# Copying the own bank first: ScalarE's copy and VectorE's add change places in a Strassen-Winograd MLP on Trainium2

## The chip, the cores and the metric

The kernel runs on one NeuronCore of a Trainium2 chip. The engines of that core are TensorE (PE, matmuls; PEld is its weight load), VectorE (DVE), ScalarE (ACT), GpSimd (POOL) and SyncE (SP), and 16 DMA engines move data. The metric is the device time of one execution in microseconds; lower is better. "Before" is the kernel as it stood, "after" the changed one.

## What is computed

One inference step of a two-layer decoder trunk: 1024 prompt tokens and 8 sample tokens, width 1024. Layer 0 mixes tokens with a recurrent block, layer 1 with sliding-window attention; each is followed by an MLP of width 4096. The change lies in the MLP, which is most of the time:

```python
D_MODEL = 1024
D_FF = 4 * D_MODEL
...
def sq_relu_mlp(x, w_up, w_down):
    return jnp.square(jax.nn.relu(x @ w_up)) @ w_down
...
        yp = yp + sq_relu_mlp(rms_norm(yp, norm_mlp_g[layer]), mlp_w_up[layer], mlp_w_down[layer])
        ys = ys + sq_relu_mlp(rms_norm(ys, norm_mlp_g[layer]), mlp_w_up[layer], mlp_w_down[layer])
```

All is float32, and each product is made of three passes over a high and a low part of both operands.

## The kernel before

The 1032 tokens (T, padded) lie along the free axis, two halves of 516 (H0, H1). The MLP is written as 2x2 block products after Strassen and Winograd, with seven products in place of eight: the four blocks are even and odd row tiles of the output (tiles he and ho, in the code e and o) by the two token halves (e0, e1, o0, o1). `mlp_products` runs through a list of steps (kind, q, i): "up" pairs q = 0 to 15 of the first matmul of the MLP, then "dn" pairs of the second one, 20 per layer. A down pair covers one pair of output tiles and one chunk of the hidden tiles (`CHUNKS`, five chunks, of 3, 3, 3, 3 and 2 pairs of hidden tiles, four down pairs each). Two further pairs of hidden tiles are kept out of the scheme and done as a plain product at the end of each layer (the tail, `down_steps`, with matmuls at L226 and weights split at L165 and L166).

In each pair the products come in the order P1, P2, P6, P7, P5, P4, P3 (`ORDER`). `product` (L514 to L522) issues 24 matmuls for an up product, 18 or 12 for a down product, each 128x128 by 258 columns, into a double bank of PSUM. There are four double banks: two "G" in turn, one "X", one "Y". P1, P6, P5 and P3 of a pair accumulate in the pair's G, the shared banks, and after each of them the running sum is needed. P2 has Y to itself, P7 has X to itself, and P4 accumulates on top of P7 in X. What must be taken out of PSUM, per pair:

- L616, ScalarE: after P1 e0 <- G, after P6 o0 <- G, after P5 o1 <- G, after P3 e1 <- G.
- L618, VectorE: after P2 e0 += Y. L620, VectorE: after P5 o1 += X (that is P7). L624, VectorE: after P4 o0 += X.

P3 overwrites the sum in G that the copy after P5 reads, and P4 overwrites the P7 in X that the add at L620 reads. So in the kernel before, P3 must wait for the copy and P4 for the add.

The order of instructions on each engine is not written out: a scheduler fills each queue from the program, by readiness as it estimates it. `tc.high_priority()` draws an instruction forward (the copies at L616), and `tc.issue_after(last["copy"])` holds back the instructions in its block until the copy that was last recorded in `last["copy"]` has been placed.

Around the products other work shares the engines:

- weights: DMA on SP's queue (raw <- w_up or w_dn, L159), differences of weight tiles on VectorE (ws, L487), split into high and low part by ScalarE (L388) and VectorE (L389);
- in the down phase the sums of hidden tiles (hsum, in memory) are loaded by POOL's queue (tl <- hsum, L532, in `Ahead.fetch`) and split by ScalarE (cast, L394) and VectorE (subtract, L395) in `Ahead.split`, which stands under `issue_after(last["copy"])`. A chunk has 7 such tiles per pair of hidden tiles, fetched while the chunk before is computed;
- a finished down tile is added to memory by POOL (spill <- ho and spill <- he, L635, accumulating DMAs); in the last chunk the sum is added into the tile instead (ho <- spill, he <- spill, L637);
- for the tail, four hidden tiles of 1032 columns (loaded as hdl, split into hdh and hdl at L394 and L395) and four weight tiles (raw <- w_dn, then wh at L165 and wl at L166). The buffer of a raw tile comes free after its subtract at L166, and then SP issues the next load.

Of the kernel before, what the change touches and what calls it, by code (L numbers as in the profile page):

```python
# [13 lines left out]
ALU = mybir.AluOpType  # L14
# [45 lines left out]
def trunk(ctx: ExitStack, tc: tile.TileContext, I, O):  # L60
    nc = tc.nc
    pe, act, dve, pool, sp = nc.tensor, nc.scalar, nc.vector, nc.gpsimd, nc.sync
# [53 lines left out]
    def quarters(x):  # L116
        return x.rearrange("p (b c) -> p b c", b=2)

    def inner(d):
        return quarters(d)[:, :, 0:QT]  # L120
# [458 lines left out]
    def mlp_products(layer, tok, pw, r, spill, acc, gnext, after):  # L579
# [11 lines left out]
        for n, (kind, q, i) in enumerate(PROG):  # L591
# [13 lines left out]
            z = st[q]  # L605
# [3 lines left out]
            d = z["g"] if i in (1, 5, 6) else z[7] if i == 4 else z.get(i, z["g"])  # L609
            product(d, alone, wt, (tok if up else ahead).ops[x] if up else ahead.ops[q // 4][x])  # L610
            e, o, g = z["e"], z["o"], inner(z["g"])
            e0, e1, o0, o1 = [quarters(t[:, h]) for t in (e, o) for h in (H0, H1)]
            if i in (1, 6, 5) or i == 3:
                t, f = {1: (e0, g), 6: (o0, g), 5: (o1, g), 3: (e1, inner(d))}[i]
                with tc.high_priority():
                    last["copy"] = act.copy(t, f).ins  # L616
            if i == 2:
                dve.tensor_tensor(e0, inner(d), e0, ALU.add)  # L618
            elif i == 5:
                dve.tensor_tensor(o1, inner(z[7]), o1, ALU.add)  # L620
                if 3 in z:
                    dve.tensor_tensor(e1, g, e1, ALU.add)
            elif i == 4:
                dve.tensor_tensor(o0, inner(d), o0, ALU.add)  # L624
            ready = {4: "o", 3: "" if alone else "e", 5: "e" if 3 in z else ""}.get(i, "")
            if ready and up:
                t = z[ready]
# [4 lines left out]
            elif ready:  # L632
                m, t = 2 * (q % 4) + (ready == "o"), z[ready]
# [577 lines left out]
    def mlp(layer, r, spill, gnext, after):  # L1211
        swap_banks(f"pu{layer}")
        return mlp_products(layer, rs.pop("tok"), rs.pop(layer), r, None, spill, gnext, after)
# [147 lines left out]
```

## Time and profile before

| | us |
|---|---|
| median of 3 runs | 2075.74 (2073.16 to 2076.03) |
| profiled execution | 2076.53 |
| its span, first to last instruction | 2074.7 |
| TensorE busy in it | 2027.6 |
| up pairs of layer 0 and 1 | about 299 and 300 |
| down pairs of layer 0 and 1 | about 289 and 284 |
| tails | about 17 and 20 |

The mean granted clock of TensorE was 0.993 of full speed. In the slices of the page TensorE is at nine tenths or more nearly throughout. In the two up phases (380 to 679 us and 1426 to 1726 us) and the two down phases (679 to 968 and 1726 to 2010) its busy time is within 1 us of the stretch, since the ends of matmuls are modelled; a late start shows as a longer group of matmuls, and in the waits of the weight load (PEld). A timeline row reads: start, length from the first start to the last end of a group, engine, line, operation, out <- in, shapes, count, and in brackets how long the engine was idle before and what released it.

### The profile page before, as it was taken

What the parts mean: (1) busy time and instruction counts of PE and PEld (TensorE: products, weight loads), DVE (VectorE), ACT (ScalarE), POOL (GpSimd) and SP (SyncE); (2) the same over time, 40 slices, a digit from 0 to 9 for tenths busy, and PEclk for the clock granted to TensorE, in tenths of its full rate; (3) what the DMA queues carried; (4) which work ended last, traced back from release to release, by engine and by line L of the source; (5) the groups of instructions that cost most, each with busy time, mean ns of one, the idle gap of its engine ahead of it and who ended that gap; (6) DMA issues with size and microseconds to landing.
All of it is one profiled execution on the core that took longest, in us unless ns stands there. A gap on an engine that the chain in (4) does not pass through costs nothing.

```text
span 2074.7 us, 38720 instructions
## 1 busy us (share of the span) xinstructions
PE 2027.6 (98%) x15190; PEld 1986.7 (96%) x15190; DVE 1449.6 (70%) x2626; ACT 1093.9 (53%) x2157; POOL 382.1 (18%) x578
## 2 busy tenths in 40 slices
PE   6999999999999999999999998999999999999989
PEld 5999999999999999999999997999999999999989
DVE  6988537876766877766747878669676667676662
ACT  5476635543434655544447878545443446555450
POOL 4553100000001233221003444000000002323210
PEclk9999999999999999999999999999999999999999
DMA  5103142244436778868332322712443446887773
GB/s 172 51 14 71 53 160 86 103 147 144 147 134 213 217 205 221 228 156 202 113 87 71 93 59 79 232 59 87 165 149 133 157 170 227 223 226 204 172 183 103
DMA packets 112982, 296.48 MB, mean 143 GB/s; under 512 B 19992, under 2 KB 45088, under 8 KB 112800
## 3 DMA queue, kind: packets, MB, share of 16 engines
q1 hardware_dynamic: 56800, 127.01, 20.3%
q0 software_dynamic: 28352, 98.30, 18.2%
q10 hardware_dynamic: 27648, 68.70, 9.1%
q8 instruction: 119, 1.95, 0.4%
q14 instruction: 63, 0.52, 0.1%
HBM read 172.03 MB, written 109.25 MB: 136 GB/s over the span
## 4 chain that ended last, share of the span: by engine, by line
PE 88%; DVE 4%; ACT 3%; issue 2%; DMA 2%; POOL 1%; SPq 0%; ACTq 0%; DVEq 0%; POOLq 0%
PE bD L519 57%; PE bP L226 11%; PE bS L226 6%; PE bP L747 4%; PE bT L226 3%; PE bO L875 2%; PE bS L830 1%; PE bT L851 1%; PE bN L693 1%; PE bS L775 1%; DVE xc L1114 1%; DMA raw<-w_dn 1%; DVE wl L166 1%; DVE t L307 0%; DMA x<-xT 0%
## 5 line engine op out<-in xcount | busy, mean ns | idle before, releaser
L519 PE MATMUL bD<-op,op 128*128 128x258 f32 x5376 | 654.1, 283 | 1.4 <-ACT ho L616 1.4
L519 PEld LDWEIGHTS bD<-op,op 128*128 128x128 f32 x5376 | 649.0, 189 | 6.2 <-ACT ho L616 5.7
L519 PE MATMUL bD<-tl,op 128*128 128x258 f32 x4704 | 580.5, 285 | 8.8 <-ACT ho L616 8.8
L519 PEld LDWEIGHTS bD<-tl,op 128*128 128x128 f32 x4704 | 572.4, 190 | 16.6 <-ACT ho L616 15.8
L532 POOL DMA_DIRECT2D tl<-hsum x196 | 118.7, 738 | 850.6 <-ACT op L388 781.5
L389 DVE TENSOR_TENSOR op<-ws,op 128x512 fp32r<-128x512 f32 (+2 forms) x288 | 170.5, 600 | 112.6 <-ACT op L388 112.4
L616 ACT COPY he<-bD 128x516 f32<-128x516 f32 x144 | 84.9, 591 | 264.8 <-PE bD L519 264.6
L388 ACT CAST op<-ws 128x512 fp32r<-128x512 f32 (+2 forms) x288 | 156.7, 549 | 124.0 <-PE bD L519 78.7
L616 ACT COPY ho<-bD 128x516 f32<-128x516 f32 x144 | 84.9, 590 | 178.4 <-PE bD L519 167.7
L395 DVE TENSOR_TENSOR tl<-tl 128x516 fp32r<-128x516 f32 x196 | 128.8, 691 | 62.9 <-ACT tl L394 62.7
L388 ACT CAST op<-raw 128x512 fp32r<-128x512 f32 (+2 forms) x216 | 114.7, 549 | 43.2 <-PE bD L519 20.1
L389 DVE TENSOR_TENSOR op<-raw,op 128x512 fp32r<-128x512 f32 (+2 forms) x216 | 125.6, 598 | 9.6 <-ACT op L388 6.8
L394 ACT CAST tl<-tl 128x516 fp32r<-128x516 f32 x196 | 116.6, 627 | 7.8 <-DMA tl<-hsum 6.3
L624 DVE TENSOR_TENSOR ho<-bD,ho 128x516 f32<-128x516 f32 x72 | 50.0, 695 | 96.7 <-PE bD L519 96.6
L166 DVE TENSOR_TENSOR wl<-raw,wh 128x1024 fp32r<-128x1024 f32 (+1 forms) x57 | 67.5, 1189 | 38.7 <-ACT wh L165 33.8
L635 POOL DMA_DIRECT2D spill<-ho x32 | 28.6, 893 | 283.4 <-DVE ho L624 280.9
L842 POOL TENSOR_SCALAR se<-se,den 128x256 f32<-128x256 f32 (+1 forms) x128 | 68.8, 551 | 64.4 <-DVE den L839 60.2
L165 ACT CAST wh<-raw 128x1024 fp32r<-128x1024 f32 (+1 forms) x60 | 58.6, 990 | 34.4 <-DMA raw<-w_in 11.3
L620 DVE TENSOR_TENSOR ho<-bD,ho 128x516 f32<-128x516 f32 x72 | 49.8, 692 | 32.2 <-ACT ho L616 32.0
L837 ACT ACTIVATE se<-se,den 128x257 f32<-128x257 f32 (+1 forms) x128 | 63.5, 500 | 13.9 <-DVE den L834 13.2
L272 ACT ACTIVATE sq<-y 128x344 f32<-128x344 f32 x48 | 23.6, 491 | 79.7 <-DVE y L355 66.8
L618 DVE TENSOR_TENSOR he<-bD,he 128x516 f32<-128x516 f32 x72 | 49.9, 692 | 22.1 <-PE bD L519 21.1
(309 smaller groups left out, 3940.9 us busy)
## 6 DMA issues: line engine op xcount, KB each, us to landing
tl<-hsum POOLq DMA_DIRECT2D x196, 258.0 KB, 8.4
raw<-w_up SPq DMA_DIRECT2D x64, 512.0 KB, 4.5
raw<-w_dn SPq DMA_DIRECT2D x64, 384.0 KB, 6.0
spill<-he POOLq DMA_DIRECT2D x32, 516.0 KB, 9.0
spill<-ho POOLq DMA_DIRECT2D x32, 516.0 KB, 6.9
hsum<-ho ACTq DMA_DIRECT2D x28, 516.0 KB, 2.7
hsum<-he ACTq DMA_DIRECT2D x28, 516.0 KB, 2.7
hsum<-ts ACTq DMA_DIRECT2D x28, 516.0 KB, 3.0
```

What stands on the lines that cost most here:

```text
L166: eng.tensor_tensor(r_(lo[:, sl]), raw[:, sl], hi[:, sl], ALU.subtract)
L226: pe.matmul(o, lhsT=r_(wt[:, col(k):col(k) + P]), rhs=r_(xt[:, cs(c)]), start=(k == 0 and a == 0), stop=(k == nk - 1 and a == 2))
L388: act.copy(r_(t[:, 0:n]), src)
L389: dve.tensor_tensor(r_(t[:, n:2 * n]), src, t[:, 0:n], ALU.subtract)
L394: act.copy(r_(hi), lo)
L395: dve.tensor_tensor(r_(lo), lo, hi, ALU.subtract)
L519: pe.matmul(d[:, 512 * b:512 * b + QT], lhsT=r_(wt[:, j * P:j * P + P]), rhs=r_(xt[:, QT * b:QT * b + QT]), start=first and j == 0 and a = ...
L532: pool.dma_start(t[:, n:2 * n], src)
L616: last["copy"] = act.copy(t, f).ins
L747: pe.matmul(ps[c], lhsT=r_(wt[:, k * P:k * P + P]), rhs=r_(xt[:, cs(c)]), start=(k == 0 and a == 0), stop=(k == M8 - 1 and a == 2))
L837: act.activation(se[:, u, 256 - n:257], se[:, u, 256 - n:257], AF.Exp, scale=-1.0, bias=dn[:, u:u + 1], accum_out=dn[:, 2 + u:3 + u])
L842: pool.tensor_scalar(e, e, dn[:, 2 + u:3 + u], 0.0, ALU.mult, ALU.add)
```

## The change

After P7, and no more after P5, ScalarE copies into o1, and it copies P7's own banks. After P5 VectorE adds the shared banks G to o1, where it added P7's banks before. The sum is the same. The copy after P7 is now the one that is recorded in `last["copy"]` at that step, and none is recorded at P5.

```diff
--- before.py
+++ after.py
@@ -610,14 +610,14 @@
             product(d, alone, wt, (tok if up else ahead).ops[x] if up else ahead.ops[q // 4][x])
             e, o, g = z["e"], z["o"], inner(z["g"])
             e0, e1, o0, o1 = [quarters(t[:, h]) for t in (e, o) for h in (H0, H1)]
-            if i in (1, 6, 5) or i == 3:
-                t, f = {1: (e0, g), 6: (o0, g), 5: (o1, g), 3: (e1, inner(d))}[i]
+            if i in (1, 6, 7, 3):
+                t, f = {1: (e0, g), 6: (o0, g), 7: (o1, inner(d)), 3: (e1, inner(d))}[i]
                 with tc.high_priority():
                     last["copy"] = act.copy(t, f).ins
             if i == 2:
                 dve.tensor_tensor(e0, inner(d), e0, ALU.add)
             elif i == 5:
-                dve.tensor_tensor(o1, inner(z[7]), o1, ALU.add)
+                dve.tensor_tensor(o1, g, o1, ALU.add)
                 if 3 in z:
                     dve.tensor_tensor(e1, g, e1, ALU.add)
             elif i == 4:
```

No instruction is added or removed, but queues are filled in another order. Three places show it. The first is TensorE's queue in an up pair, from the end of P5 to P3. The first row is the end of P5; bD549 are the pair's shared banks G, bD557 its X, bD566 the G of the next pair; "waits" names the engines whose semaphores are waited for. Before:

```order
L519 MATMUL bD549_3962<-op538_3742,op556_4062 128x258 x6
L519 MATMUL bD566_4190<-op448_3146,op561_4124 128x258 x6
L519 MATMUL bD566_4190<-op456_3192,op561_4124 128x258
L519 MATMUL bD549_3962<-op497_3480,op558_4091 128x258 [waits Activation_49]
L519 MATMUL bD549_3962<-op497_3480,op558_4091 128x258 x5
L519 MATMUL bD557_4066<-op541_3799,op554_3996 128x258 [waits DVE_49]
L519 MATMUL bD557_4066<-op541_3799,op554_3996 128x258 x5
L519 MATMUL bD557_4066<-op542_3803,op554_3996 128x258 x6
L519 MATMUL bD557_4066<-op543_3807,op554_3996 128x258 x6
L519 MATMUL bD557_4066<-op544_3811,op554_3996 128x258 x6
L519 MATMUL bD549_3962<-op498_3483,op558_4091 128x258 x6
L519 MATMUL bD549_3962<-op499_3486,op558_4091 128x258 x6
```

After:

```order
L519 MATMUL bD549_3962<-op538_3743,op556_4062 128x258 x6
L519 MATMUL bD557_4066<-op541_3801,op554_3996 128x258 [waits Activation_49]
L519 MATMUL bD557_4066<-op541_3801,op554_3996 128x258 x5
L519 MATMUL bD557_4066<-op542_3805,op554_3996 128x258 x6
L519 MATMUL bD557_4066<-op543_3809,op554_3996 128x258 x6
L519 MATMUL bD557_4066<-op544_3813,op554_3996 128x258 x6
L519 MATMUL bD549_3962<-op497_3480,op558_4092 128x258 [waits DVE_49]
L519 MATMUL bD549_3962<-op497_3480,op558_4092 128x258 x5
L519 MATMUL bD549_3962<-op498_3483,op558_4092 128x258 x6
L519 MATMUL bD549_3962<-op499_3486,op558_4092 128x258 x6
L519 MATMUL bD549_3962<-op500_3489,op558_4092 128x258 x6
L519 MATMUL bD566_4190<-op448_3146,op561_4124 128x258 x6
```

Before, part of the next pair's P1 (bD566) stands ahead of P3, and P4 (op541 to op544) stands inside P3 (op497 to op500); P3 waits for ScalarE and P4 for VectorE. After, P4 follows P5 and waits for ScalarE, and P3 follows P4 and waits for VectorE.

The second is VectorE's queue in a down pair, around the add at L620. ho2521 is the pair's odd tile, bD2519 its G, bD2528 its X, and tl2517 and tl2526 are tiles loaded from hsum. Before:

```order
L389 TENSOR_TENSOR op2564_22025<-raw2530_21785,op2564_22025 128x384 [waits DMAHW7_49,Activation_49]
L487 TENSOR_TENSOR ws2565_22054<-raw2513_21606,raw2530_21785 128x384 [waits PE_49]
L487 TENSOR_TENSOR ws2565_22054<-ws2565_22054,raw2513_21606 128x384 [waits DVE_49]
L620 TENSOR_TENSOR ho2521_21664<-bD2528_21741,ho2521_21664 128x516 [waits DMASW4_49,Activation_49]
L395 TENSOR_TENSOR tl2526_21717<-tl2526_21717 128x516 [waits DMASW6_49,Activation_49]
L624 TENSOR_TENSOR ho2521_21664<-bD2528_21741,ho2521_21664 128x516 [waits PE_49]
```

After:

```order
L389 TENSOR_TENSOR op2556_21960<-ws2541_21867,op2556_21960 128x384 [waits Activation_49]
L395 TENSOR_TENSOR tl2517_21659<-tl2517_21659 128x516 [waits DMASW3_49,Activation_49]
L395 TENSOR_TENSOR tl2526_21717<-tl2526_21717 128x516 [waits DMASW6_49,Activation_49]
L620 TENSOR_TENSOR ho2521_21664<-bD2519_21662,ho2521_21664 128x516 [waits DMASW4_49,PE_49]
L389 TENSOR_TENSOR op2562_21994<-raw2513_21606,op2562_21994 128x384 [waits DMAHW6_49,Activation_49]
L389 TENSOR_TENSOR op2564_22025<-raw2530_21785,op2564_22025 128x384 [waits DMAHW7_49,Activation_49]
L487 TENSOR_TENSOR ws2565_22054<-raw2513_21606,raw2530_21785 128x384
L624 TENSOR_TENSOR ho2521_21664<-bD2528_21741,ho2521_21664 128x516 [waits PE_49]
```

Before, the subtract of the tile tl2526 came after the add L620; after, it stands directly ahead of it, and so does that of tl2517. In ScalarE's queue the casts of the two tiles stand behind the copy of P7's banks, which is now the last copy.

The third is ScalarE's queue in the last down pair of layer 1. he2702 and ho2703 are the pair's tiles, bD2701 its G, bD2709 its X, wh2716 and wh2718 the third and fourth weight tile of the tail. Before:

```order
L616 COPY ho2703_23219<-bD2701_23217 128x516 [waits PE_49]
L394 CAST hdh2662_22895<-hdl2661_22894 128x1032 [waits DMASW3_49]
L165 CAST wh2718_23356<-raw2715_23350 128x1024 [waits DMAHW7_49]
L616 COPY ho2703_23219<-bD2701_23217 128x516 [waits PE_49]
L616 COPY he2702_23218<-bD2701_23217 128x516 [waits PE_49]
L1335 UNCONDITIONAL_BRANCH
```

After:

```order
L165 CAST wh2716_23352<-raw2696_23175 128x1024 [waits DMAHW6_49]
L616 COPY ho2703_23219<-bD2701_23217 128x516 [waits PE_49]
L394 CAST hdh2662_22896<-hdl2661_22895 128x1032 [waits DMASW3_49]
L616 COPY ho2703_23219<-bD2709_23276 128x516 [waits PE_49]
L165 CAST wh2718_23356<-raw2715_23350 128x1024 [waits DMAHW7_49]
L616 COPY he2702_23218<-bD2701_23217 128x516 [waits DVE_49,PE_49]
L1335 UNCONDITIONAL_BRANCH
```

Before, the cast wh2718 stood ahead of the copy into o1; after, it stands behind it. The cast wh2716 stands ahead of the copy after P6 in both.

At the same place, on VectorE, in the pair before that one: ho2687 is that pair's odd tile, wl2712 the low part of the tail's first weight tile. Before:

```order
L166 TENSOR_TENSOR wl2712_23343<-raw2680_23042,wh2711_23342 128x1024 [waits DVE_49,Activation_49]
L620 TENSOR_TENSOR ho2687_23086<-bD2693_23143,ho2687_23086 128x516 [waits Activation_49]
L395 TENSOR_TENSOR hdl2657_22875<-hdl2657_22875,hdh2658_22876 128x1032 [waits DMASW2_49,Activation_49]
L624 TENSOR_TENSOR ho2687_23086<-bD2693_23143,ho2687_23086 128x516 [waits PE_49]
L166 TENSOR_TENSOR wl2714_23347<-raw2695_23173,wh2713_23346 128x1024 [waits Activation_49]
L618 TENSOR_TENSOR he2702_23218<-bD2700_23216,he2702_23218 128x516 [waits PE_49,Activation_49]
```

After:

```order
L620 TENSOR_TENSOR ho2687_23086<-bD2685_23084,ho2687_23086 128x516 [waits PE_49,Activation_49]
L395 TENSOR_TENSOR hdl2657_22875<-hdl2657_22875,hdh2658_22876 128x1032 [waits DMASW2_49,Activation_49]
L624 TENSOR_TENSOR ho2687_23086<-bD2693_23143,ho2687_23086 128x516 [waits PE_49]
L166 TENSOR_TENSOR wl2712_23343<-raw2680_23042,wh2711_23342 128x1024 [waits DVE_49,Activation_49]
L166 TENSOR_TENSOR wl2714_23347<-raw2695_23173,wh2713_23346 128x1024 [waits Activation_49]
L618 TENSOR_TENSOR he2702_23218<-bD2700_23216,he2702_23218 128x516 [waits PE_49,Activation_49]
```

The subtract wl2712 moved from ahead of the adds L620 and L624 of this pair to behind both.

## Rows read from the trace of the kernel before

**Rows 1.** Page: busy us (share) xcount; the costliest group of instructions and its mean
```profile
PE 2027.6 (98%) x15190; PEld 1986.7 (96%) x15190; DVE 1449.6 (70%) x2626; ACT 1093.9 (53%) x2157; POOL 382.1 (18%) x578
...
L519 PE MATMUL bD<-op,op 128*128 128x258 f32 x5376 | 654.1, 283 | 1.4 <-ACT ho L616 1.4
```

**Rows 2.** Waits of PEld, whole span: us in total, times, longest
```profile
PEld bD L519 <- ACT ho L616: 21.5, 67, 5.6
```

**Rows 3.** Waits of PEld in 380:679, 679:968 and 1726:2010, one row each
```profile
PEld bD L519 <- ACT ho L616: 2.9, 13, 0.9
...
PEld bD L519 <- ACT ho L616: 3.3, 20, 0.2
...
PEld bD L519 <- ACT ho L616: 3.6, 19, 0.6
```

**Rows 4.** Timeline of PE near 626 and 636 us: start, length, what, count
```profile
625.72 3.52 PE L519 MATMUL bD<-op,op 128*128 128x258 f32 x28
...
635.82 2.91 PE L519 MATMUL bD<-op,op 128*128 128x258 f32 x21
```

**Rows 5.** Timeline, 635:638.5, the add after P5
```profile
636.88 0.70 DVE L620 TENSOR_TENSOR ho<-bD,ho 128x516 f32<-128x516 f32 x1 [0.80 <-ACT ho L616]
```

**Rows 6.** Timeline of PE, 674:714, last up pair [idle before <-releaser]
```profile
677.77 6.05 PE L519 MATMUL bD<-op,op 128*128 128x258 f32 x48 [0.68 <-ACT ho L616]
```

**Rows 7.** Timeline, 1921:1948, two down pairs
```profile
1926.74 0.59 ACT L616 COPY ho<-bD 128x516 f32<-128x516 f32 x1 [0.32 <-PE bD L519]
...
1930.67 0.70 DVE L624 TENSOR_TENSOR ho<-bD,ho 128x516 f32<-128x516 f32 x1 [2.13 <-PE bD L519]
...
1931.67 0.89 POOL L635 DMA_DIRECT2D spill<-ho  x1 [11.31 <-DVE ho L624]
...
1933.45 1.98 POOL L532 DMA_DIRECT2D tl<-hsum  x3
...
1942.07 0.59 ACT L616 COPY ho<-bD 128x516 f32<-128x516 f32 x1 [0.50 <-PE bD L519]
...
1942.98 0.63 ACT L394 CAST tl<-tl 128x516 fp32r<-128x516 f32 x1 [0.32 <-DMA tl<-hsum]
...
1943.75 0.68 DVE L395 TENSOR_TENSOR tl<-tl 128x516 fp32r<-128x516 f32 x1
```

**Rows 8.** L532's loads in 679:931, 1726:1976: who waited (us, times)
```profile
  ACT tl L394: 2.0, 7
...
  ACT tl L394: 4.3, 10
```

**Rows 9.** Timeline, 1898:1923, the end of a chunk
```profile
1911.47 0.59 ACT L616 COPY ho<-bD 128x516 f32<-128x516 f32 x1 [1.16 <-PE bD L519]
...
1912.48 4.00 ACT L394 CAST tl<-tl 128x516 fp32r<-128x516 f32 x6 [0.41 <-DMA tl<-hsum]
```

**Rows 10.** Timelines of both tails; windows view, 968:977 (before GB/s: clock, DMA share)
```profile
972.29 4.71 PE L519 MATMUL bD<-tl,op 128*128 128x258 f32 x24 [3.01 <-ACT ho L616]
...
2019.89 1.04 ACT L165 CAST wh<-raw 128x1024 fp32r<-128x1024 f32 x1 [5.12 <-DMA raw<-w_dn]
2020.84 0.58 ACT L616 COPY ho<-bD 128x516 f32<-128x516 f32 x1
...
2021.47 4.57 PE L519 MATMUL bD<-tl,op 128*128 128x258 f32 x24 [5.40 <-ACT ho L616]
...
968.00:977.00 9.00, 5.99 (x37) 5.77 (x36) 4.46 (x5) 2.58 (x3) 0.00 (x0) 0.81 0.86 235
```

**Rows 11.** Timeline, 1995:2032, the pair before; landing of L159's loads
```profile
2005.68 0.59 ACT L616 COPY ho<-bD 128x516 f32<-128x516 f32 x1
...
2006.96 4.56 SPq L159 DMA_DIRECT2D raw<-w_dn  x2
...
2013.22 0.59 ACT L616 COPY ho<-bD 128x516 f32<-128x516 f32 x1 [1.37 <-PE bD L519]
...
DMA to landing us min/median/max: 3.5/6.1/8.7
```

## The prediction

> **What bounds the kernel now.** First the page's busy times [rows 1]: TensorE is busy for 98% of the span, VectorE for 70% and ScalarE for 53%. Nothing that the latter two save by themselves can show; a change here is worth what it takes from TensorE's waits. Second, the list of those waits [rows 2]: the product loop (L519) is stopped by one releaser alone, ScalarE's copy into ho (L616), 67 times and for 21.5 us. Third, where: 13 times in the up pairs of layer 0, 20 and 19 times in the down pairs of the two layers [rows 3]; layer 1's up pairs show the same row as layer 0's. What is left of the 21.5 us are two long waits at the ends of the two MLPs [rows 10].
>
> Which copy is it? At the places of [rows 4 to 7] and [rows 9] it is the one after P5: P3 writes the shared banks, so it must wait until ScalarE has copied the sum out of them. The scheduler has drawn six or seven matmuls of the next pair's P1 and some of P3 around the hole.
>
> What one such wait costs is read from the pace of the matmuls. Undisturbed, 28 matmuls take 3.52 us [rows 4]; less 0.28 for the last one's own length (L519's mean, [rows 1]) that is 3.24/27 = 0.120 us each. The 21 around a P5 copy take 2.91 us: 2.63 - 20 x 0.120 = 0.23 us lost. I use 0.22.
>
> **The change, part by part.** No instruction comes or goes: 144 copies and 72 adds as before, of the same shapes. What moves is which of them stands where. The o1 copy now follows P7 and runs beside P5; the add follows P5. P4, which writes P7's banks, waits only for that early copy, which takes 0.59 us [rows 7] and has the whole of P5 as cover (24, 18 or 12 matmuls, 2.9, 2.2 or 1.4 us at 0.120). P3 waits for the add, 0.70 us [rows 5], and has the whole of P4 as cover, equally long. The order shows P5, P4, P3 on TensorE without a piece of P1 between.
>
> *Up pairs.* 12 short gaps per layer (13 waits less the long one [rows 3]): 24 x 0.22 = 5.3 us. The last up pair has no next P1 to put into the hole and stands still for 0.68 us between matmuls [rows 6], 0.9 us between weight loads [rows 3]; I take 0.9: two of them, 1.8 us. VectorE's add of 0.70 us is done early in the 2.9 us of P4: nothing takes the gap's place. Sum 7.1 us.
>
> *Down pairs, the gaps.* 39 waits [rows 3], 39 x 0.22 = 8.6, and the one of 0.6 us gives 0.4 more: 9.0 us. In the last chunk (12 matmuls, 1.4 us of cover) the add still has 0.6 us to spare.
>
> *Down pairs, what takes their place.* The splits of the loaded sums (ScalarE's cast L394, VectorE's subtract L395) are issued after the last copy. The last copy is now that of P7, so the order puts cast and subtract of a freshly loaded tile *ahead* of the add on VectorE, where before they stood behind it. P3 now waits for a DMA. In the pair of [rows 7] P5's copy starts at 1942.07 and the load lands at 1942.98, 0.91 us later. From there: cast 0.63, subtract 0.68 and the add of 0.70, one behind the other: 2.0 us, against 2.17 us of P4. Left as it is, P3 would stand still for 0.91 + 2.0 - 2.17 = 0.75 us; at a chunk's end, where the first of six tiles lands 1.01 us after P5's copy [rows 9], 0.85 us. There the casts of the next weights also stand behind six casts of tiles (4.00 us), which I price at 0.4 us more for P1, 6 such places. ScalarE sat waiting for such a load 10 times in one layer and 7 in the other [rows 8]. Bound from above: 17 x 0.85 + 2.4 = 17 us.
>
> But the loads also start sooner. The spill of ho was issued 1931.67 - 1926.74 = 4.93 us after P5's copy [rows 7], 1.0 after its add (L624) began. P4 now ends 2.2 us after P5: spill at 3.3, 1.6 us sooner. The loads were issued 6.71 us after P5's copy, behind P3 and its spill; P3 is now done six matmuls of P1 and one gap sooner, 6 x 0.120 + 0.22 = 0.9 us. With all of that the stalls are gone: bound from below 0. Loads are behind two accumulating spills on the same queue, so I take half of the 0.9 as reaching the landing: 0.35 us left of each, 17 x 0.35 = 6.0 us. Net of the down pairs: 9.0 - 6.0 = 3.0 us.
>
> That a queue cannot step past a waiting instruction is in the trace: the tail's cast of 2019.89 had waited 5.12 us for its weights, and P5's copy, for which TensorE stood idle, came only behind it, at 2020.84 [rows 10]. The Trainium skill, "TensorE: Matmul & The Clock Gate", section "Architectural detail", says the same of ScalarE and VectorE (strictly first in, first out) and so speaks against this edit: by that rule, the trace agreeing, the new stalls are as above; if the queues could reorder they would be 0.
>
> *The two tails.* In the last down pair of layer 1 ScalarE waits for the fourth weight load of the tail ahead of P5's copy (cast at 2019.89, copy at 2020.84 [rows 10]), and layer 0 has the same order: TensorE idles 3.01 and 5.40 us, and its next 24 matmuls take 4.71 and 4.57 us instead of 2.9 [rows 10]; the granted clock of the first stretch was 0.81 [rows 10], so part of it ran at the lower level of 1.2 GHz, behind the idle time. All of it together is 8.4 + 3.5 = 11.9 us, the upper bound. After the change the copy stands ahead of that cast. What is late next: the subtracts of the first two tail weights (L166) now stand behind the second add of the pair before (L624). They free the buffers of the third and fourth load, so the third, issued 1.3 us after P5's copy in that pair (2006.96 against 2005.68 [rows 11]), comes some 2.4 us later. Then it runs beside the two accumulating loads of he and ho. Of the two loads of this stretch the first landed after 3.5 us and the second, beside them, after 8.7 [rows 11]. And its cast stands ahead of P6's copy, for which P5 waits. At worst that is 2.4 + 5.2 = 7.6 us late, of which 1.7 are slack (landing at 2006.96 + 3.5, a cast of 1.04, and P6's copy at 2013.22 [rows 11]): 5.9 us of a new wait and 2.4 at the fourth weights, against 7.1 and 4.8 us won: -1.2 and -3.5, -4.7 us. Between -4.7 and 11.9 I take 3.2 us, below the middle, since the slow landing of [rows 11] is the nearer row.
>
> The same two landings show that loads of one queue are slowed by another's. The Trainium skill, "Trainium Kernel Development and Optimization", section "Key Constraints", says that transfers of all queues run on the same 16 engines and interleave. By that the third load is slow and the tails give 3.2 us; if it had engines of its own, they would give nearly the 11.9.
>
> **Sum.** 7.1 + 3.0 + 3.2 = 13.3 us. The profiled execution took 2076.5 us (span 2074.7 and 1.8 around it), so 2063.2; the median of the three runs lies 0.8 us below it: 2062.4 us. With all terms at their best it is 7.1 + 9.0 + 11.9 = 28.0 us, 2047.7; at their worst 7.1 - 8.0 - 4.7 = -5.6, 2081.3.
>
> **The rivals.** (1) *Everything closes.* The loads come 0.9 to 1.6 us sooner and no add waits for one; of the tails, half or more is won: 16.1 + 6 to 16.1 + 11.9, so 2047.7 to 2053.6, middle 2051. For it: the shift of the spill is larger than the lateness of both rows. Against: the spills and loads share engines, and the tail's load is late. Chance 0.20.
>
> (2) *Nothing to see.* The gaps close, and the new waits and the tails take it back: stalls of 0.85 at every late load (14.5 us) with tails near 0 leave 1.6 us: 2072 to 2079, middle 2074. For it: TensorE is busy for 98% already, and ends of matmuls are modelled. A form of it is that the edit does not do what it says, because the scheduler keeps its order; the order of the new kernel speaks against that. Chance 0.20.
>
> (3) *Slower.* VectorE's add stands behind the subtract of a tile that is not there yet: place, the down pairs of chunks 0 to 3; price, landing + 2.0 - 2.17 us for each. The other terms win 7.1 + 9.0 + 3.2 = 19.3 us; over 17 late loads it decides from a mean stall of 19.3/17 = 1.1 us on, and for 0.2% more (4.2 us) from 1.4 us. With landings half a us later than in the trace (a stall delays the spill, the next loads land later again) and the 0.4 at six chunk ends it is 17 x 1.35 + 2.4 = 25.4 us: 2081.8 us. Against: each late P3 also delays the next pair, so lateness does not pile up. Chance 0.09.
>
> **How the numbers follow.** Forecast 0.51 (its own range 2055 to 2071), rival 1 0.20, rival 2 0.20, rival 3 0.09. A difference of 0.2% (4.2 us) is about what a measurement of this kernel can tell from none: faster is below 2071.6, slower above 2079.9. Faster 0.51 + 0.20 = 0.71; same 0.20; slower 0.09. The range takes in the forecast, most of rival 1 and the near side of rival 2: 2049 to 2074, with rival 3 and most of rival 2's upper half left out.
>
> **What the profile after would show.** Up pairs: no row of TensorE waiting for ho L616 between 380 and 679 us, and the two 0.68 us stops gone; if a wait for VectorE (L620) stands there, the cover of P4 was misjudged. Down pairs: waits of TensorE for L620, each behind L395 and a load; 17 of about 0.35 us would be right, none is rival 1, 1 us or more each is rival 3. Chunk ends: P1 waiting for op casts (L388). Tails: the stop at P5's copy gone, a shorter one before P5 or at the tail's first matmuls (L226). The prediction is wrong in kind if the small gaps stay under another name, and wrong in size if the tails keep or lose all of their 11.9 us.

## The result, and the profile after

The changed kernel took 2060.75 us (2059.68 to 2063.82, 4 runs) against 2075.89 us (2073.16 to 2076.43, 4 runs): a ratio of 0.9932, 95% interval 0.9919 to 0.9945, 15.1 us between the medians. The forecast was 2062.4 us, with a range of 2049 to 2074, and a gain of over 0.2% with a chance of 0.71.

The page (busy us, share, count) and the list of weight-load waits, whole span, of the changed kernel, beside [rows 1, 2]:

```profile
PE 2011.6 (98%) x15190; PEld 1980.1 (96%) x15190; DVE 1441.4 (70%) x2626; ACT 1088.2 (53%) x2157; POOL 380.2 (18%) x578
...
PEld bD L519 <- ACT ho L616: 6.3, 2, 3.4
PEld bD L519 <- DVE ho L620: 6.2, 11, 1.1
```

67 waits for ScalarE's copy have become 2, of 6.3 us in place of 21.5. In their stead VectorE's add (L620) is waited for 11 times, 6.2 us. The share of TensorE's busy time did not move; as before it hides the whole story.

Where the time went is best read by stretches. For each I take the time from its first matmul's start to the first start of the next stretch, less the number of its matmuls times the undisturbed 0.1204 us: what is left was lost. (0.1204 us is the mean step from one matmul's start to the next in e14_both below, over the 2016 matmuls of chunks 0 to 3, where nothing is waited for.) All numbers are us of one profiled execution.

| stretch | before | after | gain | forecast |
|---|---|---|---|---|
| up pairs, both layers | 8.2 | 0.9 | 7.2 | 7.1 |
| down chunks 0 to 3, layer 0 | 4.2 | 0.6 | 3.6 | |
| down chunks 0 to 3, layer 1 | 4.6 | 7.0 | -2.4 | |
| last chunk without its last pair, both | 1.9 | -0.1 | 1.9 | |
| all these down pairs | 10.7 | 7.5 | 3.1 | 3.0 |
| last down pair, layer 0 | 4.7 | 4.3 | 0.4 | |
| last down pair, layer 1 | 7.1 | 3.5 | 3.6 | |
| both last pairs | 11.8 | 7.8 | 4.0 | 3.2 |

The sum is 14.3 us. The spans differ by 2074.7 - 2057.9 = 16.8; most of the rest lies before the first product (1.0) and between the layers (1.4), where the program is the same. That it is scatter is not shown, but other kernels with the same program there differ as much: 354.7 to 356.0 us before the first product in all kernels below, and 424.3 to 427.4 between the layers in those that leave the tail's weights alone.

**Up pairs.** Timeline of TensorE around 626 us, the stretch of [rows 4]: start, length, count.

```profile
625.78 14.45 PE L519 MATMUL bD<-op,op 128*128 128x258 f32 x119
```

119 matmuls without a hole, (14.45 - 0.28)/118 = 0.120 us each; between 378 and 676 us the list of waits holds no row of L519.

**Down pairs.** Timeline around an add in layer 1 (start, length, engine, line, idle before and releaser), and who waited for the tiles' loads in 676:922 and 1712:1960, beside [rows 7, 8]; the last row is the add's waits in 676:922:

```profile
1882.74 0.62 ACT L394 CAST tl<-tl 128x516 fp32r<-128x516 f32 x1 [2.03 <-DMA tl<-hsum]
...
1883.40 0.70 DVE L395 TENSOR_TENSOR tl<-tl 128x516 fp32r<-128x516 f32 x1 [1.96 <-ACT tl L394]
...
1884.01 0.69 DVE L620 TENSOR_TENSOR ho<-bD,ho 128x516 f32<-128x516 f32 x1
...
1884.76 15.45 PE L519 MATMUL bD<-tl,op 128*128 128x258 f32 x126 [0.87 <-DVE ho L620]
...
  ACT tl L394: 4.6, 10
...
  ACT tl L394: 15.1, 11
...
PEld bD L519 <- DVE ho L620: 0.4, 2, 0.2
```

The chain is the forecast one: the load lands, ScalarE casts the tile (1882.74), VectorE subtracts (1883.40) and only then adds (1884.01). At 1884.76 TensorE starts P3 after 0.87 us of idling for the add. At another stop of this kernel (0.83 us, at 1868.45) a weight's subtract (L389, 0.55 us) stands between L395 and the add as well. ScalarE waited 15.1 us for loads in layer 1, 4.3 before, and 4.6 in layer 0. In layer 0 the add is waited for twice (0.4 us), so the other nine waits, 5.8 us, are layer 1's. No row of P1 waiting for casts of weights (L388) is in the list: the 2.4 us that the worst case had at the chunk ends did not appear.

**The tails.** Timelines of the two last down pairs, as in [rows 10], and of the loads ahead of layer 1's, as in [rows 11]:

```profile
959.49 1.04 ACT L165 CAST wh<-raw 128x1024 fp32r<-128x1024 f32 x1 [4.69 <-DMA raw<-w_dn]
...
961.08 6.11 PE L519 MATMUL bD<-tl,op 128*128 128x258 f32 x36 [2.60 <-ACT ho L616]
...
1993.03 0.69 DVE L620 TENSOR_TENSOR ho<-bD,ho 128x516 f32<-128x516 f32 x1 [0.59 <-PE bD L519]
...
1996.63 1.46 SPq L159 DMA_DIRECT2D raw<-w_dn  x2
...
2003.23 1.04 ACT L165 CAST wh<-raw 128x1024 fp32r<-128x1024 f32 x1 [5.34 <-DMA raw<-w_dn]
2004.18 0.58 ACT L616 COPY ho<-bD 128x516 f32<-128x516 f32 x1
...
2004.82 4.60 PE L519 MATMUL bD<-tl,op 128*128 128x258 f32 x36 [3.24 <-ACT ho L616]
...
DMA to landing us min/median/max: 6.6/8.2/9.8
```

The stop has moved from P3 to P5: 2.60 us for 3.01 in layer 0, 3.24 for 5.40 in layer 1. The cast ahead of the blocked copy (2003.23, copy of P6 at 2004.18) is that of the third tail weight and not of the fourth.

### The profile page after: what moved, and what is told of

It reads as the page before. It is cut to its first block, busy times and chain, and to the rows that moved or that the text cites. A ratio compares the mean times of both kernels' runs of the same rounds, so it can differ in the third digit from the quotient of the medians.

```text
span 2057.9 us, 38784 instructions
## 1 busy us (share of the span) xinstructions
PE 2011.6 (98%) x15190; PEld 1980.1 (96%) x15190; DVE 1441.4 (70%) x2626; ACT 1088.2 (53%) x2157; POOL 380.2 (18%) x578
## 4 chain that ended last, share of the span: by engine, by line
PE 82%; issue 6%; DVE 4%; ACT 3%; DMA 2%; POOL 2%; SPq 0%; ACTq 0%; POOLq 0%; DVEq 0%
PE bD L519 51%; PE bP L226 11%; PE bS L226 6%; PE bP L747 4%; PE bT L226 3%; PE bO L875 2%; DMA tl<-hsum 1%; PE bS L830 1%; PE bT L851 1%; PE bN L693 1%; PE bS L775 1%; DVE xc L1114 1%; POOL spill L635 1%; POOL tl L532 1%; DMA raw<-w_dn 1%
## 5 line engine op out<-in xcount | busy, mean ns | idle before, releaser
L519 PE MATMUL bD<-op,op 128*128 128x258 f32 x5376 | 648.2, 283 | 0.0
L519 PEld LDWEIGHTS bD<-op,op 128*128 128x128 f32 x5376 | 647.7, 190 | 0.3
L519 PE MATMUL bD<-tl,op 128*128 128x258 f32 x4704 | 572.2, 284 | 9.9 <-ACT ho L616 5.8
L519 PEld LDWEIGHTS bD<-tl,op 128*128 128x128 f32 x4704 | 569.0, 190 | 12.9 <-ACT ho L616 6.3
L532 POOL DMA_DIRECT2D tl<-hsum x196 | 117.1, 686 | 846.4 <-DMA hsum<-he 387.1
L389 DVE TENSOR_TENSOR op<-ws,op 128x512 fp32r<-128x512 f32 (+2 forms) x288 | 170.1, 598 | 120.8 <-ACT op L388 120.5
L395 DVE TENSOR_TENSOR tl<-tl 128x516 fp32r<-128x516 f32 x196 | 128.3, 691 | 92.3 <-ACT tl L394 89.2
L388 ACT CAST op<-ws 128x512 fp32r<-128x512 f32 (+2 forms) x288 | 155.8, 550 | 59.8 <-DVE op L389 34.3
L389 DVE TENSOR_TENSOR op<-raw,op 128x512 fp32r<-128x512 f32 (+2 forms) x216 | 123.9, 597 | 61.8 <-ACT op L388 61.2
L388 ACT CAST op<-raw 128x512 fp32r<-128x512 f32 (+2 forms) x216 | 113.5, 548 | 33.3 <-PE bD L519 18.8
L394 ACT CAST tl<-tl 128x516 fp32r<-128x516 f32 x196 | 116.7, 626 | 21.6 <-DMA tl<-hsum 19.7
L629 ACT ACTIVATE ho<-ho 128x1032 f32<-128x1032 f32 x32 | 34.2, 1070 | 106.7 <-DVE ho L628 106.7
L624 DVE TENSOR_TENSOR ho<-bD,ho 128x516 f32<-128x516 f32 x72 | 49.7, 690 | 20.5 <-PE bD L519 20.5
L226 PE MATMUL bP<-hh,wh 128*128 128x344 f32 x216 | 55.4, 327 | 8.0 <-ACT hh L1050 7.7
```

Source lines behind the costliest of these rows:

```text
L226: pe.matmul(o, lhsT=r_(wt[:, col(k):col(k) + P]), rhs=r_(xt[:, cs(c)]), start=(k == 0 and a == 0), stop=(k == nk - 1 and a == 2))
L388: act.copy(r_(t[:, 0:n]), src)
L389: dve.tensor_tensor(r_(t[:, n:2 * n]), src, t[:, 0:n], ALU.subtract)
L394: act.copy(r_(hi), lo)
L395: dve.tensor_tensor(r_(lo), lo, hi, ALU.subtract)
L519: pe.matmul(d[:, 512 * b:512 * b + QT], lhsT=r_(wt[:, j * P:j * P + P]), rhs=r_(xt[:, QT * b:QT * b + QT]), start=first and j == 0 and a = ...
```

## The experiments

Each experiment was timed against the kernel before on the same chip (2075.16 us beside e1, e2, e3 and e6; 2076.14 beside e5, e9, e10 and e11; 2075.44 beside e12, e13 and e14; 2074.09 beside e8). Lost time by stretches, as above (the column "start" is the stop between the last up and the first down product, both layers; the last chunk without its last pair is left out, it lost 0.1 us at most in every changed kernel but e1 with 1.8, e10 with 13.3 and e11 with 15.6):

| kernel | us | ratio | up | start | c0-3, L0 | c0-3, L1 | last pair, L0 | L1 |
|---|---|---|---|---|---|---|---|---|
| before | 2075.89 | 1 | 8.2 | 0 | 4.2 | 4.6 | 4.7 | 7.1 |
| after | 2060.75 | 0.9932 | 0.9 | 0 | 0.6 | 7.0 | 4.3 | 3.5 |
| e1_up_only | 2067.09 | 0.9965 | 0.8 | 0 | 4.2 | 4.0 | 3.4 | 7.2 |
| e2_down_only | 2074.23 | 0.9998 | 8.8 | 0 | 3.4 | 9.0 | 2.9 | 4.2 |
| e3_add_first | 2064.98 | 0.9959 | 0.8 | 0 | 3.6 | 6.8 | 2.9 | 4.3 |
| e5_swap | 2064.83 | one run | 0.9 | 0 | 1.7 | 8.5 | 4.8 | 4.5 |
| e6_tail_raw | 2065.23 | 0.9955 | 1.1 | 0 | 1.6 | 7.2 | 0.0 | 7.4 |
| e8_small_spill | 2053.06 | one run | 0.9 | 0 | 0.0 | 0.2 | 4.5 | 3.0 |
| e9_split_later | 2066.84 | 0.9959 | 0.9 | 8.2 | 3.3 | 2.3 | 4.6 | 5.6 |
| e10_tail_early | 2156.50 | 1.0386 | 1.0 | 0 | 44.9 | 46.9 | 2.3 | 2.3 |
| e11_later_and_tail | 2173.44 | 1.0468 | 1.0 | 8.2 | 49.2 | 47.5 | 2.3 | 2.3 |
| e12_later_but_first | 2054.15 | 0.9898 | 1.1 | 0 | 0.0 | 0.0 | 2.9 | 3.1 |
| e13_tail_raw_a | 2058.62 | 0.9920 | 1.1 | 0 | 3.2 | 6.2 | 0.0 | 0.0 |
| e14_both | 2049.61 | 0.9878 | 0.8 | 0 | 0.0 | 0.0 | 0.0 | 0.1 |

### One half of the change alone: e1_up_only and e2_down_only

```diff
-            if i in (1, 6, 7, 3):
-                t, f = {1: (e0, g), 6: (o0, g), 7: (o1, inner(d)), 3: (e1, inner(d))}[i]
+            first_own = up          # e2: not up
+            if i in (1, 6, 7 if first_own else 5, 3):
+                t, f = {1: (e0, g), 6: (o0, g), 7: (o1, inner(d)), 5: (o1, g), 3: (e1, inner(d))}[i]
...
-                dve.tensor_tensor(o1, g, o1, ALU.add)
+                dve.tensor_tensor(o1, g if first_own else inner(z[7]), o1, ALU.add)
```

> Only the up pairs copy the own bank first; the down pairs stand as in the kernel before. Theory (gains add up stage by stage, and the up pairs have no new wait): 7.2 us faster than before, 2068.7 us (2067.5 to 2070), the up stretches each 3.6 us shorter, the last down pair of each layer still losing 4.7 and 7.1 us. Rival (the gain of the full change comes from the tails or from outside the MLP): 2073 to 2076 us.

Measured: 2067.09 us, ratio 0.9965 (0.9952 to 0.9979), which is 7.3 us by the ratio; the median lies 0.4 us below the stated range. The up stretches lost 0.8 us in place of 8.2, the down chunks what they lost before. The up term stands by itself.

> Only the down pairs copy the own bank first; the up pairs stand as before. Theory: the rest of the gain, 15.1 - 7.2 = 7.9 us, of it 1.2 in chunks 0 to 3, 1.9 in the last chunk, 4 at the tails and some scatter: 2068 us (2066.5 to 2070); waits of TensorE for the add L620 some 6 us in layer 1, none to speak of in layer 0. Rival (a gain only comes when both phases change): above 2072 us.

Measured: 2074.23 us, ratio 0.9998 (0.9989 to 1.0007): no gain that can be told from none. The expectation failed, and the time lies where its rival had it (above 2072). The rival's reason, that both phases must change, does not hold for the up pairs (e1). The waits of the weight load, whole span:

```profile
PEld bD L519 <- ACT ho L617: 11.5, 28, 2.9
PEld bD L519 <- DVE ho L621: 10.0, 15, 1.9
```

15 waits for the add (L621 here), 10.0 us, where the full change had 11 and 6.2. In the table chunks 0 to 3 lose 12.4 us against 7.6, and all down pairs 19.5 against 22.5 before: 3.0 us won, where the full change won 3.1 + 4.0. Between the layers 1.1 of the 3.0 are given back (427.0 us from layer 0's last product to layer 1's first, 425.9 before). The order of these pairs is nearly that of the full change (in layer 0's chunks 0 to 3, 304 of VectorE's 316 instructions and 261 of ScalarE's 269 stand in the same order). The size of the new waits differs from one execution to another: 12.4, 10.4, 10.2, 9.4, 8.8 and 7.6 us in e2, e3, e5, e13, e6 and the full change, each from one trace, and in e5 the queues of these chunks stand in the full change's order throughout. That the two halves add up to less than the whole by some 6 us (7.3 and 0.4 by the ratios, against 14.1, each uncertain by 2 to 3) is explained by rows only for 5 of them, and what sets the size was not found.

### Holding back VectorE's subtract: e3_add_first

```diff
-                dve.tensor_tensor(o1, g, o1, ALU.add)
+                last["add"] = dve.tensor_tensor(o1, g, o1, ALU.add).ins
...
-            with tc.issue_after(last["copy"]):
+            with tc.issue_after(last["copy"]), tc.issue_after(last["add"]):
```

> The full change, with one edge more: the subtracts of loaded tiles (L395) are held behind VectorE's add after P5. Theory (the new waits of the down pairs come from the add standing behind a subtract that waits for its load): the waits for L620 are gone, 7 us of excess in layer 1's chunks 0 to 3 fall below 1, and the time is 6 to 7.5 us below the full change: 2053.3 to 2054.8 us. Rival (the loads themselves are too late for the work behind them, whatever the order): the same us turn up as waits for L395, L394 or the casts of weights, 2058 to 2062 us.

Measured: 2064.98 us, ratio 0.9959 (0.9946 to 0.9971), and 12 waits for the add, 9.5 us. The expectation failed, and so did my account of the wait. The time lies above the rival's range too, though the rival named the casts of weights, at which the wait turns up. Timeline of a late pair in layer 1, with P7's copy as its first row:

```profile
1864.85 0.59 ACT L616 COPY ho<-bD 128x516 f32<-128x516 f32 x1 [0.65 <-PE bD L519]
1867.96 0.62 ACT L394 CAST tl<-tl 128x516 fp32r<-128x516 f32 x1 [2.52 <-DMA tl<-hsum]
1868.50 0.51 ACT L388 CAST op<-ws 128x384 fp32r<-128x384 f32 x1
...
1869.03 0.56 DVE L389 TENSOR_TENSOR op<-ws,op 128x384 fp32r<-128x384 f32 x1 [4.05 <-ACT op L388]
...
1869.98 0.69 DVE L620 TENSOR_TENSOR ho<-bD,ho 128x516 f32<-128x516 f32 x1
...
1870.72 1.48 PE L519 MATMUL bD<-tl,op 128*128 128x258 f32 x10 [1.59 <-DVE ho L620]
```

The subtract L395 no longer stands ahead of the add, but the cast L394 still stands ahead of two casts of weights (L388) on ScalarE. It waits 2.52 us for its load; VectorE idles 4.05 us for the weight cast behind it, whose subtract (L389) is ahead of the add; TensorE idles 1.59 us. The split blocks the add over either queue, so its place on ScalarE has to move too.

### Splitting later: e9_split_later and e12_later_but_first

The constant 4 in `Ahead.split` is the number of products between a tile's fetch and its split. In e9 it is 6, so that a tile fetched at a pair's end is split behind the next P5; in e12 it is 6 but for the first chunk:

```diff
-                while self.raw and self.raw[0][0] <= step - 4:
+                while self.raw and self.raw[0][0] <= step - (4 if self.raw[0][1] == 0 else 6):
```

> The full change, with the split of a loaded tile issued six products after its fetch and not four, so that ScalarE's cast too stands behind the copy after P3 where it stood ahead of casts of weights on which VectorE's queue, and in it the add after P5, hung. Theory (the new wait is the place of the split in both queues, and holding back the subtract alone only handed it to the cast): the 7.6 us of excess in chunks 0 to 3 (0.6 and 7.0) fall below 2 in sum, 5 to 7 us below the full change, 2053.5 to 2056 us. Rival (the tiles come too late for their own products or the DMA engines are simply full): the excess stays above 5 us, 2059 us or more.

Measured: 2066.84 us, ratio 0.9959 (0.9946 to 0.9971): too slow for the theory, and in the rival's range. As the rival has it, tiles came too late for their own products, but only in the first chunk, and by the place of their cast and not by their load. The waits of the weight load, whole span, and TensorE at the start of layer 0's down phase:

```profile
PEld bD L519 <- ACT tl L394: 8.3, 2, 4.2
...
PEld bD L519 <- ACT ho L616: 5.9, 2, 3.0
...
682.96 0.60 ACT L394 CAST tl<-tl 128x516 fp32r<-128x516 f32 x1
...
683.62 8.56 PE L519 MATMUL bD<-tl,op 128*128 128x258 f32 x46 [3.95 <-ACT tl L394]
```

No wait for the add L620 is left in either layer. But the first chunk's tiles are needed at once and are now cast too late: 3.95 us of standstill per layer, and 46 matmuls behind it in 8.56 us in place of 5.7 (45 x 0.12 + 0.28). The cast at 682.96 shows no wait for a load; the granted clock of 683.6 to 692 us was 0.63.

> The full change, with the split six products after the fetch for the later chunks only; the first chunk's tiles, which the down pairs need at once, are split after four as in the full change. Theory: the stop of 4.1 us at the start of each down phase, with the slow matmuls behind it, is gone, and so are the waits for the add L620: excess of chunks 0 to 3 under 1.5 us in sum of both layers (7.6 in the full change), 5.5 to 7.5 us below the full change, 2053.2 to 2055.2 us. Rival (the later split only hands the wait on, to the products that use the tiles): 2058 us or more.

Measured: 2054.15 us, ratio 0.9898 (0.9884 to 0.9911); 0.0 us lost in chunks 0 to 3 of both layers. The waits of the weight load, whole span, as far as they are L519's:

```profile
PEld bD L519 <- ACT ho L616: 5.9, 2, 3.1
```

As expected: the new wait was the place of the split in the queues, and it is gone. The loads did not get faster: POOL's queue stands in the full change's order in chunks 0 to 3, and from issue to landing (minimum, median, maximum, in 676:922 and 1712:1960) it took

```profile
DMA to landing us min/median/max: 4.9/7.6/10.2
...
DMA to landing us min/median/max: 4.7/7.6/10.5
```

against medians of 7.2 and 7.5 us in the full change.

### Why the loads are late: e8_small_spill and e5_swap

e8 leaves 1024 of 1032 columns out of the accumulating spills, so nearly all of their traffic is gone. VectorE's and ScalarE's queues of chunks 0 to 3 stay in the full change's order; in POOL's the spill of he now stands behind the first load of a pair and not ahead of it:

```diff
-                    pool.dma_start(acc[m], t, accum_op=ALU.add)
+                    pool.dma_start(acc[m][:, 0:8], t[:, 0:8], accum_op=ALU.add)
```

> The full change, with the accumulating spills of the down tiles cut to 8 of 1032 columns (the sums over chunks are then incomplete); all queues but the order of the two spills of a pair stand as in the full change. Theory (the loads land late because they share the DMA engines with the two spills ahead of them): loads land some 5 to 6 us after their issue and not 7 to 10, no wait for the add L620 is left in either layer, the time falls by 6 to 8 us to some 2053 to 2055 us. Rival (the loads are late because they are issued late, behind P3's spill): landings and waits for L620 stay, 5 us or more in sum.

Time from issue to landing of the tiles' loads (minimum, median, maximum) in 676:922 of the kernel before, of the full change and of e8, then the same three in layer 1 (from 1712 on):

```profile
DMA to landing us min/median/max: 4.9/8.7/10.9
...
DMA to landing us min/median/max: 4.9/7.2/9.4
...
DMA to landing us min/median/max: 2.9/4.1/7.0
...
DMA to landing us min/median/max: 4.3/8.8/11.0
...
DMA to landing us min/median/max: 4.8/7.5/10.5
...
DMA to landing us min/median/max: 3.3/4.7/6.7
```

Measured: 2053.06 us, no wait for L620 left, landings after 4.1 and 4.7 us in the median against 7.2 and 7.5. So the spills make the loads late. By which way is not told apart. Of the loads that ScalarE's cast waits for, the first ones behind a pair's spills, seven in each layer can be set side by side: in e8 they landed after 3.5 to 5.7 us in place of 7.5 to 10.3, but they also left 1.5 to 2.1 us sooner, measured from the next P5's end. By these numbers either alone would have ended these waits. The rows of before show that the full change made the median landing 1.5 and 1.3 us shorter, but the longest one 1.5 us shorter in layer 0 and only 0.5 in layer 1, where the waits are.

> The full change, with the two layers' areas of memory for the sums (hsum) exchanged. One cause for new waits in layer 1 only (where the area lies): layer 0 gets 5 to 7 us of excess in chunks 0 to 3 and layer 1 under 2. The other (what else runs in layer 1, or the moment at which its loads fall): 0.6 and 7 us as in the full change.

```diff
-            self.sums = hsum[layer]
+            self.sums = hsum[1 - layer]
...
-                    stores.append(sums_of(e, o, hsum[layer][q]))
+                    stores.append(sums_of(e, o, hsum[1 - layer][q]))
```

Measured: 2064.83 us (one run), 1.7 us lost in layer 0 and 8.5 in layer 1. Most of the waits stay in layer 1; where the sums lie is not the cause. Why layer 1 has the later loads stays open, and the difference is one of degree: in e2, e3 and e13 layer 0 lost 3.2 to 3.6 us there too. One thing is to be seen in the weights' loads (full change; 676:922, then 1712:1960): they land sooner in layer 1, the tiles' loads do not.

```profile
DMA to landing us min/median/max: 3.3/6.4/6.9
...
DMA to landing us min/median/max: 3.1/4.3/7.3
```

### The tails: e6_tail_raw, e13_tail_raw_a and e10_tail_early

The third and fourth weight tile get a buffer that is not the first two's, in the pool of split weights (e6) or in that of activations (e13):

```diff
+            elif name[:2] == "ds" and units[len(raws)][1] >= 2:
+                raws.append(W("raw"))          # e13: A("raw")
```

> The full change, with the third and fourth weight load of each tail landing in buffers of another pool, so that they need not wait for the subtracts of the first two. Theory (TensorE's stop ahead of P5 of the last pair comes from the cast of the third tail weight, which waits for its late load ahead of P6's copy on ScalarE): stops of 2.6 and 3.2 us gone, the slow matmuls behind them too, 6 to 8 us below the full change: 2052.8 to 2054.8 us. Rival (the loads only move and then hold up the loads of tiles or the fetch of the sums, or the stop goes to the tail's first matmuls): 2058 to 2061 us.

Measured: 2065.23 us, ratio 0.9955 (0.9943 to 0.9968). Layer 0's last pair lost nothing any more, layer 1's 7.4 us. What layer 0 won came back behind it: from its last product to layer 1's first it took 428.6 us against 424.6, 2.9 of these 4.0 in the tail, which now waited for its weights, as told for e13 below. Timeline in layer 1, with the two loads:

```profile
1983.29 16.16 SPq L161 DMA_DIRECT2D raw<-w_dn  x2
...
2008.16 1.04 ACT L167 CAST wh<-raw 128x1024 fp32r<-128x1024 f32 x1 [4.58 <-DMA raw<-w_dn]
2009.11 0.58 ACT L618 COPY ho<-bD 128x516 f32<-128x516 f32 x1
...
2009.75 5.41 PE L521 MATMUL bD<-tl,op 128*128 128x258 f32 x24 [4.87 <-ACT ho L618]
...
L161 SPq DMA_DIRECT2D raw<-w_dn x2: 327/328/328, 1983.3 to 1999.1; - x2
```

The third load left at 1983.3, the fourth only at 1999.1: its buffer in that pool was still taken (SP waited for matmuls that read it, from 1987.6 on). Its cast stood ahead of P7's copy, and TensorE idled 4.87 us. The cause is the expected one, at the other load; the remedy was poor.

> The full change, with the third and fourth weight load of each tail landing in free tiles of the pool that holds activations. Theory (the two loads come late because they wait for buffers, and their casts stand ahead of copies): both last down pairs lose less than 1 us (4.3 and 3.5 in the full change), 5 to 7.5 us below the full change, 2053.2 to 2055.7 us. Rival (a load early enough collides with the tiles' loads, or its cast holds up another copy, as with the other pool): 2058 us or more.

Measured: 2058.62 us, ratio 0.9920 (0.9908 to 0.9933). Both last pairs lose nothing, as expected, but the time falls less and lies in the rival's range. In layer 0 the tail itself now waits for its weights. The weight load's waits of the whole span for the add, and those in 940:1000 for the tail's weights (line numbers are 2 higher):

```profile
PEld bD L521 <- DVE ho L622: 7.9, 13, 1.2
...
PEld bP L228 <- ACT wh L167: 1.9, 1, 1.9
PEld bP L228 <- DVE wl L168: 1.0, 1, 1.0
```

The full change has no such wait there. From layer 0's last product to layer 1's first it takes 427.3 us against 424.6 (starts in the two timelines): of the 4.3 us won in layer 0, 2.7 come back as the 2.9 us of waits for the weights that follow. Chunks 0 to 3 were 1.8 us worse in this execution (9.4 against 7.6).

> The full change, with the four weight tiles of each tail loaded and split ahead of the down pairs and not within the last ones. Theory (the tails lose their time to the third and fourth weight load, whose casts stand ahead of copies): the last down pairs lose nothing (4.3 and 3.5 us in the full change), 7 to 8 us below the full change, 2052.5 to 2054.5 us. Rival (the work only moves: splits at the start of the down pairs delay casts there by as much): 2058 us or more.

```diff
+        add_units(f"ds{layer}", I["w_dn"][layer][8 * len(CHUNKS):], 4, lambda j: W)
         for b in range(4 * len(CHUNKS)):
...
-        add_units(f"ds{layer}", I["w_dn"][layer][8 * len(CHUNKS):], 4, lambda j: W)
```

Measured: 2156.50 us, ratio 1.0386 (1.0372 to 1.0401), 80 us slower. Waits of the weight load:

```profile
PEld bD L519 <- ACT op L388: 57.6, 48, 1.4
PEld bD L519 <- ACT ho L616: 35.5, 40, 1.0
```

The tail's eight tiles lie in the pool of 12 buffers in which the down weights are split (op, L388). With them there from the start of the down phase four are left, and TensorE waits for a weight cast 48 times. That the one comes from the other is read from the code; no run gave the pool more buffers. Neither the theory nor the rival had that.

> Both: split six products after the fetch, and the tail's weights ahead of the down pairs. Theory (two separate causes, gains add): 12 to 15 us below the full change, 2046 to 2049 us. Rival (one of the two waits hides the other): less than 9 us below it, over 2052 us.

e11 is e9 with this edit, 2173.44 us, ratio 1.0468 (1.0454 to 1.0482): it carries both faults and tells nothing of its own question.

### Both remedies: e14_both

e12's and e13's edits together.

> Both: split six products after the fetch but for the first chunk, and the tail's loads in free tiles. Theory (two separate causes, gains add): 11 to 14 us below the full change, 2046.5 to 2049.5 us. Rival (one hides the other): above 2052 us.

Measured: 2049.61 us (2048.83 to 2050.33), ratio 0.9878 (0.9862 to 0.9893), 25.8 us below its before by the medians and 4.5 below e12; the forecast range ended 0.1 us lower. The group of down matmuls on its page (busy, mean ns | idle before):

```profile
L521 PE MATMUL bD<-tl,op 128*128 128x258 f32 x4704 | 566.8, 283 | 0.0
```

TensorE never idles ahead of one. The gains add: 11.1 us below the full change, where e12 alone has 6.6 and e13 alone 2.1 (8.7 together); each of these is uncertain by 2 to 3 us. Layer 0's tail waits for its weights as in e13 (2.0 and 1.0 us). This is faster than both kernels, and lies where the first rival had its time (2047.7 to 2053.6).

## Why the prediction was right, and where it was not

- **Up pairs**, 7.1 us forecast, 7.2 seen, and e1 shows it alone. Reading the cost of one gap from the pace of matmuls around it (0.22 us) and counting gaps in the list of waits was enough; P4 covers the add with time to spare, as worked out.
- **Down pairs**, 3.0 us forecast, 3.1 seen, but from two terms that were both too small by some 1.6 us: 10.7 won (9.0 forecast) and 7.6 lost (6.0). That the difference came out is luck. The mechanism, an add behind the split of a tile that has not landed, is shown by e12 (split moved, loads as late as before, wait gone); in e8 (loads sooner, wait gone) it shows from the other side. Two steps of it failed. The price was put at 0.35 us on each of 17 late loads; there were 11 waits with a mean of 0.56, nine of them in layer 1, and e2, with the same down pairs, had 12.4 us lost in these chunks. And the place was put on VectorE's queue alone; e3 shows that ScalarE's cast blocks the add as well, over the weights' casts.
- **The half of 0.9 us** by which I let landings come sooner was a choice between bounds. The seven loads of each layer that are compared under e8 landed, in the mean, 0.99 us after the next P5's end before the change and 0.41 after it in layer 1: 0.6 us sooner, near the half of 0.45. In layer 0 they came 1.5 us sooner, from 0.72 us after that end to 0.82 ahead of it. So layer 0 was priced too high (7 x 0.35 = 2.5 us, and 0.6 were lost in chunks 0 to 3) and layer 1 too low (10 x 0.35 = 3.5, and 7.0 were lost). That the sum of the two came near is luck.
- **Tails**, 3.2 us forecast, 4.0 seen. The stop moved ahead of P5, onto the cast of the third tail weight, as said. Its load was issued 3.6 us after P5's end (1996.63, the add at 1993.03) for 1.3 before: 2.3 us later, 2.4 forecast. It landed after 6.6 us, between the 3.5 and 8.7 of [rows 11]. e6 and e13 show the cause by moving the loads. The mechanism was right; the 3.2 was a point taken between -4.7 and 11.9, so that it came near is a choice that went well and not a working.
- **The rivals.** "Everything closes" did not happen by itself, but e14 makes it happen. "Slower" had the right mechanism and the wrong price: a mean of 1.1 us on 17 loads was needed. e2 comes closest to "nothing to see": there chunks 0 to 3 lost 12.4 us, 3.6 more than before, against what the last chunk and the tails won.

## What to carry to other kernels

Give the early result to the engine that can take it while the next product runs, and let the late one be covered by the product after; but ask of every instruction that moves ahead of the late one whether it waits for a DMA, on each queue by which the late one can be reached. A scheduling anchor (here the last copy) that moves with an edit moves all that hangs on it: after this edit a constant of 4 had to become 6 (but for the first chunk), worth 6.6 us more. When a cast that waits for a load stands in an engine's queue ahead of a copy out of PSUM, price the load and not the cast.

## What was not expected of the hardware

- The same steps of the program had loads landing at another pace in the two layers: weights in a median of 6.4 us in layer 0 and 4.3 in layer 1 (6.9 and 4.9 before the change), while the long waits for tiles were layer 1's. Exchanging the areas of the sums left the order as it was (6.4 and 5.1, e5). With the spills cut the two layers were alike (3.3 and 3.4, e8), so the difference goes with the spills; more is not known.
- Matmuls behind a stop are not always slow. After 2.60 us of idling in layer 0's last pair 36 matmuls took 6.11 us, after 3.24 us in layer 1's 36 took 4.60. The granted clock of the two stretches (the last three numbers of a row are the clock, the DMA share and GB/s) was 0.84 and 1.00:

```profile
957.00:968.00 11.00, 8.40 (x56) 8.19 (x55) 6.16 (x6) 5.66 (x7) 0.87 (x1) 0.84 0.79 216
2001.00:2011.00 10.00, 6.76 (x53) 6.55 (x53) 4.90 (x5) 4.62 (x6) 0.21 (x1) 1.00 0.53 143
```

So behind the shorter stop part of the stretch ran at the lower level of 1.2 GHz, and behind the longer one none did; between these two stops the length alone does not decide it.
